# Hybrid backbone layer on one core: the output projection's operand is stored already split in high and low parts

## The chip, the cores and the metric

The kernel runs on one core of one Trainium2 chip. The metric is the device time of one execution in microseconds. TensorE does the matrix products, VectorE (DVE in the rows) and ScalarE (ACT) the elementwise work, GpSimd (POOL) some elementwise work and some DMA issues, SyncE (SP) nearly all DMA issues. Both weights and activations lie in DRAM as float32.

## The reference, cut to what matters

One layer over 1024 latent tokens and 256 context tokens of width 1024. Of the first of its two sub-layers, the change touches the end:

```python
lru_l, lru_c = rglru_mixer(...)                       # (1, 1024, 1024)
ssd_l, ssd_c = ssd_mixer(...)                         # ends in rms_norm(y * silu(z), norm_g)
x = x + g1 * (jnp.concatenate([lru_l, ssd_l], axis=-1) @ lp['w_out'])   # w_out: (2048, 1024)
```

Before that, one input projection feeds both mixers: an LRU (a convolution, gates, and a linear recurrence in both directions, times a GeLU gate) and an SSD (a chunked state-space scan in both directions). After it comes a gated feed-forward part with a convolution of width 3, and a final norm. All of it is computed in float32.

## The kernel before, in words

A float32 product is made of three products of a faster format, `float32r`: an operand is split into a high part (a ScalarE copy into `float32r`, line 144) and a low part (VectorE's difference of the operand and the high part, line 145), and high x high, high x low and low x high are added in PSUM. The helper is `split`. Whoever reads an operand for products therefore pays a ScalarE and a VectorE pass over it.

The work runs in stages, on a TensorE that has something to do in most of them. The times are those of the profiled execution.

- **LRU stage** (to about 490 us): 8 steps `i`, each 128 channels over all tokens. Products with `w_in` give the mixer's input and its gate; convolution (`conv4`), split into `xh` and `xl`, products for the gates (line 432), scans; then line 458 multiplies by the GeLU gate `gg`, and line 460 stores `gg` (128 channels x 1024 tokens) into the DRAM tile `mixd`, ordered by chunks of 128 tokens. Between the steps VectorE reduces adaLN weights (`ada_col`, line 180), each 512 KB, through the ring `wraw` of three buffers that also serves the weights.
- **SSD preparation** (490 to about 742 us): the remaining columns of `w_in`, convolution, decays.
- **SSD stage** (about 742 to 941 us): for two groups of heads and 8 chunks each, states, scores and outputs (`diag`, `chunk_out`, `fwd`), which VectorE chains together. It ends each chunk by storing the gated output into the DRAM tile `gd` (line 778). As filler, `out_lru` runs beside it: the LRU half of the output projection, one column half `h` (512 columns) after the other.
- **SSD projection**: `out_half(1, 0, ...)` (about 941 to 985 us) and `out_half(1, 1, ...)` (about 985 to 1046 us), the SSD half of the output projection for the first and second 512 columns. The second also normalises the new stream (`post`) and prepares the operands `b11`, `t1`, ... of the feed-forward part.
- **Feed-forward part** (from about 1074 us) with two large products made by a Strassen-like scheme.

`out_half(half, h, src, nxt, order)` is what the change rewrites. It makes 8 weight blocks (`out_prep`: a load of 256 KB through the ring, a scaling on VectorE in lines 671 or 673, a split into `oh` and `ol`, nine buffers each, at a high priority). Then it goes over 8 chunks of 128 tokens, the first two as a pair. For each chunk it loads 512 KB of `mixd` or `gd` (through the ring; the first pair of the SSD half through the two `x1` buffers, line 685), and for each half `kq` of it (four blocks of 128) splits 128x512 into `mh` and `ml` and makes 12 products (lines 709 to 711). `mh` and `ml` have four buffers each in the LRU half, in a pool of the SSD stage, and two each in the SSD half. As each column half goes over all chunks, each mixer output is loaded twice and split twice: 2 x 2 x 8 x 2 = 64 splits of 128x512.

The framework that builds the program orders the instructions of each engine by priority in a model of its own; so work of one stage appears beside that of another. Each engine, and each DMA queue, then runs its list in order: an instruction or DMA issue that waits holds what stands behind it. A buffer is reused when the last reader of its former content is done.

The trace prints tiles without their numbers: `x<-gd` is the load of an `x1` buffer, `h<-h,h` one of `post`.

Of the kernel before, what the change touches and what calls it, by code (L numbers as in the profile page):

```python
# [7 lines left out]
FT = mybir.dt.float32  # L8
FR = mybir.dt.float32r
# [6 lines left out]
P = 128  # L16
D = 1024
KD = 8
T = 1024
NCL = 8  # L20
# [30 lines left out]
def backbone_kernel(ctx: ExitStack, tc: tile.TileContext, x, ctxt, vec, rows, ada, ada_t, w_in, w_dt,  # L51
                    gw, w_out, w_up, w_down, out, dbg=None):
    nc = tc.nc
# [6 lines left out]
    ring = ctx.enter_context(tc.tile_pool(name="ring", bufs=2))  # L60
    dram = ctx.enter_context(tc.tile_pool(name="dram", bufs=1, space=DRAM))

    mixd = dram.tile([NCL, P, KD, P], FT, name="mixd")
    gd = dram.tile([NCL, P, KD, P], FT, name="gd")
    zd = dram.tile([NCL, P, D], FT, name="zd")
    xd = dram.tile([NCH, P, D], FT, name="xd")
# [26 lines left out]
    for nm, op in (("gt", OP.is_lt), ("lt", OP.is_gt), ("le", OP.is_ge), ("ge", OP.is_le)):  # L93
        m = m2[:, 0 if nm == "le" else 1, :] if nm in ("le", "ge") else const.tile([P, P], FR, name="m_" + nm)
# [38 lines left out]
    def load_w(src, n=1024):  # L133
        raw = ring.tile([P, 1024], FT, name="wraw", bufs=3)[:, :n]
        nc.sync.dma_start(raw, src)
        return raw
# [3 lines left out]
    def split(hi, lo, src, eng_hi=None):  # L140
        if eng_hi is V:
            V.tensor_copy(hi, src)
        else:
            A.activation(hi, src, AF.Copy)  # L144
        V.tensor_tensor(lo, src, hi.bitcast(FT), op=OP.subtract)  # L145
# [223 lines left out]
    with tc.tile_pool(name="la", bufs=1, reuse_waits="tile") as la, \  # L369
# [21 lines left out]
        for i in range(KD):  # L391
# [46 lines left out]
            for d in range(2):  # L438
# [18 lines left out]
            V.tensor_tensor(hs[0], hs[0], hs[1], op=OP.add)  # L457
            V.tensor_tensor(gg.rearrange("p (c r) -> p c r", r=GR), gg.rearrange("p (c r) -> p c r", r=GR),
                            hs[0].rearrange("p (r c) -> p c r", c=GW), op=OP.mult)
            nc.sync.dma_start(mixd[:, :, i, :].rearrange("c p t -> p c t"), gg.rearrange("p (c t) -> p c t", t=P))  # L460

            ada_cols(i, 2, 5)

# [214 lines left out]
    mpool = [None]  # L678

    def out_half(half, h, src, nxt, order=tuple(range(NCL))):  # L680

        m0 = []
        for c in order[:2] if half else ():
            m0.append(ow.tile([P, D], FT, name="x1", bufs=2))
            nc.sync.dma_start(m0[-1], src[c].rearrange("p a b -> p (a b)"))
        for k in range(len(wts), KD):
            out_prep(half, h, k)
        mine = wts[:]
        wts.clear()
        for cs in [order[0:2]] + [(c,) for c in order[2:]]:  # L690
            mr = m0 or [load_w(src[c].rearrange("p a b -> p (a b)")) for c in cs]
            m0 = []
            po = [fpa.tile([P, 512], FT, name="pa" if c % 2 else "pb", bufs=2) if half
                  else ops.tile([P, 512], FT, name="pf", bufs=2) for c in cs]
            for kq in range(2):
                hl = []
                qs = slice(kq * 512, (kq + 1) * 512)
                for c, m in zip(cs, mr):
                    mp, nb = (ow, 2) if half else (mpool[0], 4)
                    mh = mp.tile([P, 512], FR, name="mh", bufs=nb)  # L700
                    ml = mp.tile([P, 512], FR, name="ml", bufs=nb)
                    split(mh, ml, m[:, qs])
                    hl.append((mh, ml))
                for j in range(4):
                    k = kq * 4 + j
                    oh, ol = mine[k]
                    for (mh, ml), p_ in zip(hl, po):
                        a, b = mh[:, j * P:(j + 1) * P], ml[:, j * P:(j + 1) * P]
                        PE.matmul(p_, a, oh, start=k == 0, stop=False)
                        PE.matmul(p_, a, ol, start=False, stop=False)  # L710
                        PE.matmul(p_, b, oh, start=False, stop=k == KD - 1)
            if nxt and cs[0] == order[-1]:
                out_prep(nxt[0], nxt[1], 0)
            for c, p_ in zip(cs, po):
                yield c, p_
# [555 lines left out]
```

## Time and profile before

| what | value |
|---|---|
| median of 3 runs | 1775.61 us (1767.23 to 1783.1) |
| the profiled execution | 1780.98 us |
| its span | 1779.2 us |
| TensorE products busy | 1624.8 us (91%) |
| VectorE busy | 1418.1 us (80%) |
| ScalarE busy | 931.2 us (52%) |
| GpSimd busy | 445.8 us (25%) |
| moved by DMA | 238.78 MB, mean 134 GB/s |

Busy shares are averages over stages with different limits, so a stage has to be looked at by itself. Matrix products are pipelined: a TensorE that is busy all the time may still issue them at different rates, and its idle time is what the other engines cost it. The idle time of any other engine costs nothing by itself. The granted clock of TensorE is a share of 2.4 GHz.

### The profile page before, as it was taken

How to read it: one execution, taken by the hardware profiler on the slowest of the kernel's cores; microseconds unless marked ns; L12 is line 12 of the kernel's file. 1: busy time of each engine (PE TensorE's matmuls, PEld its weight loads, DVE VectorE, ACT ScalarE, POOL GpSimd, SP SyncE). 2: the span in 40 equal slices, each digit the busy share in tenths (PEclk: the TensorE clock that was granted, in tenths of full speed). 3: DMA queues.
4: the chain of work that ended last, by engine and by line, in shares of the span. 5: the costliest groups of instructions: out<-in, count | busy, mean ns of one | idle time of the engine just before them, and what ended most of it. 6: DMA issues, size and time to landing. Idle time of an engine off the chain costs nothing.

```text
span 1779.2 us, 21578 instructions
## 1 busy us (share of the span) xinstructions
PE 1624.8 (91%) x7682; PEld 1311.9 (74%) x7682; DVE 1418.1 (80%) x1966; ACT 931.2 (52%) x1408; POOL 445.8 (25%) x335
## 2 busy tenths in 40 slices
PE   2889999999999999699999969899999999999996
PEld 2468787887977677476677757788888888888885
DVE  2777878786566668889895699899999999879787
ACT  3548786867746666422323573343443443445445
POOL 0000000000037767332120035445545444200000
PEclk8999999998999999899899988999999999999998
DMA  6615324241213222476756531222322223594433
GB/s 150 234 50 165 100 84 148 88 138 29 79 65 104 95 101 101 165 246 208 249 174 219 197 129 65 89 101 101 124 101 95 101 101 113 183 366 137 165 101 107
DMA packets 106764, 238.78 MB, mean 134 GB/s; under 512 B 10528, under 2 KB 33184, under 8 KB 106656
## 3 DMA queue, kind: packets, MB, share of 16 engines
q1 hardware_dynamic: 105136, 233.73, 39.7%
q0 software_dynamic: 1520, 3.67, 0.6%
q8 instruction: 60, 0.98, 0.2%
q14 instruction: 48, 0.39, 0.1%
HBM read 176.55 MB, written 60.82 MB: 133 GB/s over the span
## 4 chain that ended last, share of the span: by engine, by line
PE 40%; DVE 7%; DMA 3%; ACT 2%; issue 2%; POOL 0%; SPq 0%; POOLq 0%; DVEq 0%; ACTq 0%
PE pd L848 2%; PE pd L846 2%; PE pd L847 2%; PE pc L848 2%; PE pc L847 2%; PE pc L846 2%; PE pa L846 2%; PE pa L847 2%; PE pa L848 2%; PE pdn L1107 2%; PE pdn L1105 2%; PE pdn L1106 2%; DMA wraw<-in_w_out 2%; PE pb L846 1%; PE pb L847 1%
## 5 line engine op out<-in xcount | busy, mean ns | idle before, releaser
L558 POOL TENSOR_TENSOR rh<-m,dah 128x512 fp32r<-128x512 f32 x64 | 74.3, 1160 | 565.5 <-ACT dah L144 503.8
L159 PE MATMUL pl<-hh,whi 128*128 128x512 f32 x416 | 167.6, 403 | 2.2 <-ACT gg L414 1.9
L161 PE MATMUL pl<-hh,wlo 128*128 128x512 f32 x416 | 165.6, 398 | 0.8 <-DVE wlo L145 0.8
L160 PE MATMUL pl<-hl,whi 128*128 128x512 f32 x416 | 165.0, 397 | 0.0
L1023 DVE SCALAR_TENSOR_TENSOR cen<-u,vt,cen 128x1008 f32<-128x1008 f32 x192 | 155.3, 859 | 11.6 <-ACT cen L1019 11.6
L144 ACT ACTIVATE sh<-wraw 128x512 fp32r<-128x512 f32 x158 | 98.5, 624 | 105.7 <-PE pd L847 52.7
L145 DVE TENSOR_TENSOR sl<-wraw,sh 128x512 fp32r<-128x512 f32 x158 | 132.6, 840 | 0.0
L965 POOL TENSOR_TENSOR ssum<-wraw 128x512 f32<-128x512 f32 x48 | 70.5, 1469 | 169.8 <-DVE sl L145 147.8
L144 ACT ACTIVATE sh<-ssum 128x512 fp32r<-128x512 f32 x96 | 59.8, 627 | 101.3 <-PE pc L847 64.4
L144 ACT ACTIVATE sh<-b 128x512 fp32r<-128x512 f32 x80 | 50.6, 632 | 107.0 <-PE pdn L1106 55.3
L159 PEld LDWEIGHTS pl<-hh,whi 128*128 128x128 f32 x416 | 80.0, 192 | 19.5 <-ACT gg L414 2.1
L161 PEld LDWEIGHTS pl<-hh,wlo 128*128 128x128 f32 x416 | 79.7, 192 | 18.0 <-DVE wlo L145 2.0
L160 PEld LDWEIGHTS pl<-hl,whi 128*128 128x128 f32 x416 | 80.2, 193 | 17.2 <-issue 1.0
L1019 ACT ACTIVATE cen<-u,vt 128x1024 f32<-128x1024 f32 x48 | 59.8, 1245 | 59.7 <-DVE u L1012 32.2
L145 DVE TENSOR_TENSOR sl<-ssum,sh 128x512 fp32r<-128x512 f32 x96 | 81.7, 853 | 3.4 <-ACT sh L144 3.4
L383 PE MATMUL pl<-whi,hh 128*128 128x256 f32 x256 | 73.8, 288 | 8.8 <-DVE xc L356 5.7
L558 POOL TENSOR_TENSOR rh<-m,dal 128x512 fp32r<-128x512 f32 x64 | 77.6, 1212 | 0.0
L145 DVE TENSOR_TENSOR sl<-b,sh 128x512 fp32r<-128x512 f32 x80 | 56.0, 701 | 26.6 <-ACT sh L144 26.5
L384 PE MATMUL pl<-wlo,hh 128*128 128x256 f32 x256 | 73.4, 287 | 1.2 <-DVE wlo L145 1.2
L144 ACT ACTIVATE mh<-wraw 128x512 fp32r<-128x512 f32 x56 | 34.9, 629 | 75.3 <-PE pf L710 45.3
L385 PE MATMUL pl<-whi,hl 128*128 128x256 f32 x256 | 73.1, 285 | 0.0
L180 DVE SCALAR_TENSOR_TENSOR wraw<-wraw,silr 128x1024 f32<-128x1024 f32 x32 | 39.1, 1222 | 38.7 <-DMA wraw<-in_ada_t 38.6
(440 smaller groups left out, 5179.6 us busy)
## 6 DMA issues: line engine op xcount, KB each, us to landing
wraw<-in_w_up SPq DMA_DIRECT2D x48, 512.0 KB
wraw<-actd SPq DMA_DIRECT2D x42, 512.0 KB
wraw<-in_w_in SPq DMA_DIRECT2D x36, 512.0 KB
actd<-cen SPq DMA_DIRECT2D x33, 512.0 KB
wraw<-in_ada_t SPq DMA_DIRECT2D x32, 512.0 KB
b<-in_w_down SPq DMA_DIRECT2D x24, 512.0 KB
xk<-xd SPq DMA_DIRECT2D x38, 256.0 KB
ddd<-wd SPq DMA_DIRECT2D x32, 256.0 KB
```

Of the source, the lines that this page charges most:

```text
L144: A.activation(hi, src, AF.Copy)
L145: V.tensor_tensor(lo, src, hi.bitcast(FT), op=OP.subtract)
L159: PE.matmul(ps, wh[:, k, :], hh[k][:, t0:t0 + n], start=k == 0, stop=False)
L160: PE.matmul(ps, wh[:, k, :], hl[k][:, t0:t0 + n], start=False, stop=False)
L161: PE.matmul(ps, wl[:, k, :], hh[k][:, t0:t0 + n], start=False, stop=k == KD - 1)
L383: PE.matmul(o, hh[k][:, t], wh[:, k % 4, :], start=k == 0, stop=False)
L384: PE.matmul(o, hh[k][:, t], wl[:, k % 4, :], start=False, stop=False)
L558: G.tensor_tensor(rh, m[:, None, :].to_broadcast([P, 4, P]), sv[:, :, None].to_broadcast([P, 4, P]), op=OP.mult)
L846: PE.matmul(ps, a[0][:, ks], b[0][:, k, :], start=k == 0, stop=False)
L847: PE.matmul(ps, a[0][:, ks], b[1][:, k, :], start=False, stop=False)
L848: PE.matmul(ps, a[1][:, ks], b[0][:, k, :], start=False, stop=k == 3)
L1023: V.scalar_tensor_tensor(cen[:, o:o + m], uu[:, i_:i_ + m], w_, cen[:, o:o + m], op0=OP.mult, op1=OP.add)
```

## The change

The DRAM tile `mixd` gets a leading index for the two parts, and a new tile `gsd` of the same kind is made for the SSD outputs.

In the LRU stage, `gg` is split after line 458: the high part goes to a new tile `ghi`, the low part into `gg` itself, and two stores replace one. In the LRU half of `out_half` a chunk's two parts are loaded whole, 128x1024 each, into `mh` and `ml`, with two buffers each (before: four of half the width), with no split.

In the SSD half, the first column half loads and splits as before; each part is then also stored to `gsd` by a DMA that GpSimd issues, four of 256 KB for a chunk. The second column half loads the parts from `gsd`: chunks at even places into the two buffers of `mh` and of `ml`, by four loads of 256 KB; the chunk at place 1 into the two `x1` buffers, and the chunks at places 3, 5 and 7 into two of the ring's three buffers, by two loads of 512 KB. The loads of the first two chunks stand ahead of the weight blocks in the program.

So 64 splits of 128x512 become 16 of that size and 8 of 128x1024.

```diff
--- before.py
+++ after.py
@@ -60,7 +60,8 @@
     ring = ctx.enter_context(tc.tile_pool(name="ring", bufs=2))
     dram = ctx.enter_context(tc.tile_pool(name="dram", bufs=1, space=DRAM))
 
-    mixd = dram.tile([NCL, P, KD, P], FT, name="mixd")
+    mixd = dram.tile([2, NCL, P, KD, P], FT, name="mixd")
+    gsd = dram.tile([2, NCL, P, D], FT, name="gsd")
     gd = dram.tile([NCL, P, KD, P], FT, name="gd")
     zd = dram.tile([NCL, P, D], FT, name="zd")
     xd = dram.tile([NCH, P, D], FT, name="xd")
@@ -457,7 +458,10 @@
             V.tensor_tensor(hs[0], hs[0], hs[1], op=OP.add)
             V.tensor_tensor(gg.rearrange("p (c r) -> p c r", r=GR), gg.rearrange("p (c r) -> p c r", r=GR),
                             hs[0].rearrange("p (r c) -> p c r", c=GW), op=OP.mult)
-            nc.sync.dma_start(mixd[:, :, i, :].rearrange("c p t -> p c t"), gg.rearrange("p (c t) -> p c t", t=P))
+            ghi = lw.tile([P, T], FR, name="ghi")
+            split(ghi, gg.bitcast(FR), gg)
+            for e, t in ((0, ghi.bitcast(FT)), (1, gg)):
+                nc.sync.dma_start(mixd[e, :, :, i, :].rearrange("c p t -> p c t"), t.rearrange("p (c t) -> p c t", t=P))
 
             ada_cols(i, 2, 5)
 
@@ -679,28 +683,64 @@
 
     def out_half(half, h, src, nxt, order=tuple(range(NCL))):
 
+        def halves(n, c):
+
+            if half and not h:
+                raw = m0.pop(0) if m0 else load_w(src[c].rearrange("p a b -> p (a b)"))
+                for kq in range(2):
+                    qs = slice(kq * 512, (kq + 1) * 512)
+                    m = [ow.tile([P, 512], FR, name="m" + e, bufs=2) for e in "hl"]
+                    split(*m, raw[:, qs])
+                    for e in range(2):
+                        nc.gpsimd.dma_start(gsd[e, c][:, qs], m[e].bitcast(FT))
+                    yield m
+                return
+            if half and n % 2 == 0:
+                ms = [[ow.tile([P, 512], FR, name="m" + e, bufs=2) for e in "hl"] for _ in range(2)]
+                for kq, m in enumerate(ms):
+                    for e in range(2):
+                        nc.sync.dma_start(m[e].bitcast(FT), gsd[e, c][:, kq * 512:(kq + 1) * 512])
+                yield from ms
+                return
+            if not half:
+                m = [mpool[0].tile([P, D], FR, name="m" + e, bufs=2) for e in "hl"]
+            elif n == 1:
+                m = [ow.tile([P, D], FT, name="x1", bufs=2).bitcast(FR) for _ in "hl"]
+            else:
+                m = [ring.tile([P, 1024], FT, name="wraw", bufs=3).bitcast(FR) for _ in "hl"]
+            for e in range(2):
+                nc.sync.dma_start(m[e].bitcast(FT), gsd[e, c] if half else
+                                  src[e, c].rearrange("p a b -> p (a b)"))
+            for kq in range(2):
+                yield [t[:, kq * 512:(kq + 1) * 512] for t in m]
+
         m0 = []
-        for c in order[:2] if half else ():
+        for c in order[:2] if half and not h else ():
             m0.append(ow.tile([P, D], FT, name="x1", bufs=2))
             nc.sync.dma_start(m0[-1], src[c].rearrange("p a b -> p (a b)"))
+        its = {}
+
+        def begin(n):
+            its[n] = halves(n, order[n])
+            if h or not half:
+                its[n] = iter([next(its[n]), next(its[n])])
+
+        if half and h:
+            begin(0)
+            begin(1)
         for k in range(len(wts), KD):
             out_prep(half, h, k)
         mine = wts[:]
         wts.clear()
-        for cs in [order[0:2]] + [(c,) for c in order[2:]]:
-            mr = m0 or [load_w(src[c].rearrange("p a b -> p (a b)")) for c in cs]
-            m0 = []
+        for ns in [(0, 1)] + [(n,) for n in range(2, NCL)]:
+            cs = [order[n] for n in ns]
+            for n in ns:
+                if n not in its:
+                    begin(n)
             po = [fpa.tile([P, 512], FT, name="pa" if c % 2 else "pb", bufs=2) if half
                   else ops.tile([P, 512], FT, name="pf", bufs=2) for c in cs]
             for kq in range(2):
-                hl = []
-                qs = slice(kq * 512, (kq + 1) * 512)
-                for c, m in zip(cs, mr):
-                    mp, nb = (ow, 2) if half else (mpool[0], 4)
-                    mh = mp.tile([P, 512], FR, name="mh", bufs=nb)
-                    ml = mp.tile([P, 512], FR, name="ml", bufs=nb)
-                    split(mh, ml, m[:, qs])
-                    hl.append((mh, ml))
+                hl = [next(its[n]) for n in ns]
                 for j in range(4):
                     k = kq * 4 + j
                     oh, ol = mine[k]
```

## Rows read from the trace of the kernel before

**Rows 1.** Windows of five stretches: engines' busy time, instructions, granted clock, DMA.

```profile
core 0: us, PE busy (x) PEld busy (x) DVE busy (x) ACT busy (x) POOL busy (x), PEclk, DMA share, GB/s
150.00:490.00 340.00, 317.31 (x1807) 276.14 (x1806) 257.12 (x245) 254.25 (x262) 0.00 (x0) 0.97 0.32 102
742.00:941.00 199.00, 185.62 (x851) 134.35 (x852) 173.56 (x267) 61.66 (x120) 45.11 (x36) 0.95 0.67 217
941.00:985.00 44.00, 40.75 (x179) 32.75 (x178) 22.59 (x39) 16.43 (x32) 0.00 (x0) 1.00 0.67 225
985.00:1046.00 61.00, 55.72 (x259) 44.59 (x258) 46.07 (x95) 40.69 (x101) 3.27 (x2) 0.97 0.58 199
1046.00:1074.00 28.00, 13.01 (x51) 8.73 (x49) 27.03 (x45) 16.47 (x39) 10.19 (x7) 0.72 0.14 48
```

**Rows 2.** Groups by line, 150 to 490: busy us, mean ns, idle before.

```profile
L180 DVE SCALAR_TENSOR_TENSOR wraw<-wraw,silr 128x1024 f32<-128x1024 f32 x27 | 33.0, 1221 | 32.1 <-DMA wraw<-in_ada_t 32.0
...
L145 DVE TENSOR_TENSOR wlo<-wraw,whi 128x1024 fp32r<-128x1024 f32 x21 | 25.8, 1229 | 10.7 <-ACT whi L144 10.7
...
L144 ACT ACTIVATE whi<-wraw 128x1024 fp32r<-128x1024 f32 x21 | 22.1, 1053 | 21.9 <-PE pl L385 17.2 <-PE pg L160 4.7
```

**Rows 3.** The waits of TensorE, 150 to 490: total us, times, longest.

```profile
PE pg L432 <- ACT xh L144: 10.1, 3, 4.4
```

**Rows 4.** The groups by line, 742 to 941.

```profile
L145 DVE TENSOR_TENSOR ml<-wraw,mh 128x512 fp32r<-128x512 f32 x32 | 26.1, 831 | 5.6 <-ACT mh L144 5.1 <-PE pf L710 0.5
...
L144 ACT ACTIVATE mh<-wraw 128x512 fp32r<-128x512 f32 x32 | 19.8, 627 | 52.8 <-PE pf L710 45.3 <-DMA wraw<-mixd 4.5 <-DMA gd<-gt 3.0
```

**Rows 5.** The waits of TensorE, 742 to 941.

```profile
PE pst L775 <- DVE yy L771: 6.2, 5, 3.0
```

**Rows 6.** The chain of waits, 838 to 852: start, duration, what.

```profile
843.31 4.92 DMA wraw<-in_w_out
...
848.25 1.12 DVE wraw L673
...
849.40 0.63 ACT oh L144
850.03 0.53 ACT mh L144
...
850.60 0.80 PE pf L709
```

**Rows 7.** The chain of waits, 885 to 900.

```profile
889.50 5.43 DMA x<-gd
```

**Rows 8.** The tile actd: issue ns min/median/max, first and last start; landing.

```profile
L1039 POOL DMA_DIRECT2D actd<-cen x1: 746/746/746, 1547.1 to 1547.1; - x1
...
DMA to landing us min/median/max: 3.3/5.8/5.9
```

**Rows 9.** The groups by line of ScalarE, 941 to 985.

```profile
L144 ACT ACTIVATE mh<-wraw 128x512 fp32r<-128x512 f32 x12 | 7.6, 631 | 18.6 <-PE pb L710 12.7 <-ACT tq L837 3.9 <-PE pa L710 2.0
```

**Rows 10.** The DMA issues that GpSimd makes: KB each, median us to landing.

```profile
out<-b POOLq DMA_DIRECT2D x4, 512.0 KB, 7.3
actd<-cen POOLq DMA_DIRECT2D x3, 512.0 KB, 5.8
```

**Rows 11.** The groups by line of VectorE, 1022 to 1046.

```profile
L145 DVE TENSOR_TENSOR ml<-wraw,mh 128x512 fp32r<-128x512 f32 x6 | 4.1, 683 | 0.1
```

**Rows 12.** The waits of TensorE, 941 to 1046.

```profile
PE pb L709 <- ACT mh L144: 2.7, 2, 2.3
PE pb L711 <- DVE ml L145: 2.5, 2, 1.6
PE pa L709 <- ACT mh L144: 1.8, 1, 1.8
PE pa L711 <- DVE ml L145: 1.6, 1, 1.6
```

## The prediction

> **What bounds the kernel now.** I first read where the change acts: the split of mixer outputs runs in four stretches, so I cut the span into them and took each engine's busy time [rows 1]. TensorE is the fullest engine in the first four, but not in the same way. In the LRU stage (150 to 490 us) it is busy 317.31 of 340 us, VectorE 257.12, ScalarE 254.25. In the SSD stage, which carries the LRU half of the output projection as filler (742 to 941), TensorE has 185.62 of 199 us and VectorE 173.56: two engines close to full, with the DMA engines at 0.67. In the first column half of the SSD projection (941 to 985) TensorE has 40.75 of 44 and VectorE only 22.59. In the second (985 to 1046) TensorE has 55.72 of 61, VectorE 46.07. Then, from 1046 to 1074, TensorE falls to 13.01 of 28 and VectorE is at 27.03: it bounds the passage into the feed-forward part. The question for each stretch is therefore not how much work leaves VectorE and ScalarE, but which TensorE idle time that work ends.
>
> The profiled execution took 1780.98 us, 1.8 of it outside the span of 1779.2; the median of the runs is 1775.61. I make the sum as a difference on the profiled execution and put it on the median.
>
> **Part 1: the LRU stage gets the splits.** Each of its 8 steps gains a ScalarE copy and a VectorE subtraction of 128x1024; the same shapes take 1053 and 1229 ns for weights [rows 2]. That is 8.4 us of ScalarE and 9.8 us of VectorE in 340. Two stores replace one, 8 more on SP's queue. The cover is VectorE's idle time before the adaLN reductions, 32.1 us, nearly all waiting for their weights' transfers [rows 2]. Where the cover is gone, the added pair delays the next step's convolution and its split, for which TensorE already waits 10.1 us in 3 waits [rows 3]; then all of it counts, 8 x (1.05 + 1.23) = 18 us. Below, the bound is 0, since the stage only gains work. The scheduler puts the convolution ahead and the gated output's work into gaps, so I take about 0.5 us per step: **+4 us** (0 to +18).
>
> **Part 2: the SSD stage loses 32 splits.** They are 19.8 us of ScalarE and 26.1 us of VectorE [rows 4]. TensorE idles 199 - 185.62 = 13.4 us, so that is the most that can be won. Of its waits, 6.2 us are for VectorE's last product before the transposes [rows 5]; with 26.1 of 173.56 us gone from VectorE I take about half, 3 us. The largest single gap is at the change from the first to the second column half [rows 6]: the last `w_out` block is loaded (4.92 us), scaled, split into `oh`, and only behind that, on ScalarE's queue, stands the mixer split `mh` for which the product at 850.60 waits. Without it the products of the blocks already split need not stand behind the last block. But a new wait takes its place: a chunk's parts now need both of two buffers, which come free when the products of the chunk two places before end, not when a split ends. The parts of the second chunk of the new pair can then be asked for only at about 842, and a 512 KB load took 5.43 us in this stage [rows 7]: they are there at about 847.5, so some 3 us of the 850.60 are won. The same limit costs at the start, where four loads (2.1 MB, 6.5 us at the 324 GB/s worked out below) must follow the end of the work that held the pool's room, some 2 us later than the first product now. I count 16 more loads on SP's in-order queue as covered, because the parts need no split behind their landing; what stands behind a blocked one are the loads of x, z and the decays, for which VectorE waits. Their 8.4 MB bring the stage's 43 MB (217 GB/s x 199 us) to 52 MB, at 217 / 0.67 = 324 GB/s some 160 us of 199: no bound on average. Another 2 us I give to VectorE being less in the way elsewhere. Sum -3 - 3 + 2 - 2 = **-6 us** (-13.4 to +8: the last where both pair loads, 13 us, lie on the path and only 5 us of gains come).
>
> **Part 3: the first half of the SSD projection stores its parts.** Its 16 splits stay. Added are 32 stores of 256 KB, issued by GpSimd, which is idle here [rows 1]. An issue occupies GpSimd 0.75 us [rows 8], 4 per chunk 3.0 us, while a chunk takes TensorE 44 / 8 = 5.5 us [rows 1]: the queue keeps up. What matters is the wait: each buffer of parts (two of each kind) is now free for the next split only once its store has landed, and ScalarE, which waits there, holds behind it the squares for the norm and the weight splits. A buffer's turn is the copy, 0.63 us [rows 9], plus issue to landing. It is free of charge up to 5.5 - 0.63 = 4.9 us, less some 0.2 us of signalling, so 4.7 us. No 256 KB store of GpSimd stands in the trace: those of 512 KB took 3.3 to 5.9 us, and 7.3 for the output [rows 8, 10]. At half the size I take 4 to 5 us, just at the limit, since the DMA share here would go from 0.67 to about 0.9 with 4.2 MB more: **+2 us**. Bounds: 0 if landings stay near 3.3; at 7.3 each of 7 turns costs 7.3 - 4.7 = 2.6 us, +18.
>
> The page "DMA: Bandwidth & Descriptors" of the Trainium skill (Anatomy of one DMA) gives a GpSimd DMA about 2.0 us plus the bytes over 436 GB/s, an estimate of 2.6 us for 256 KB. By that this part would cost 0 and the sum would be 2 us lower; the rows for 512 KB, all longer than its 3.2 us, speak against relying on it.
>
> **Part 4: the second half loads what was stored.** 16 splits go, 10.9 us of VectorE and 10.1 of ScalarE at the row's 0.68 and 0.63 us [rows 9, 11]. TensorE's waits for such splits from 941 to 1046 sum to 8.6 us in four rows [rows 12]; about two thirds lie in this half (61 - 55.72 = 5.3 us idle). Six of the subtractions fall into the last stretch before 1046, 4.1 us [rows 11], where VectorE runs on into the passage and is full there [rows 1], so those shorten the passage too. Given back: 24 loads instead of 8 on SP, 4.2 MB more at a DMA share of 0.58, and the first chunk's parts can only be loaded once the first half's last buffers are free, where both chunks of the pair were loaded ahead before. A load of 5.43 us [rows 7] against weights that are being prepared in the same time costs 1 to 2 us. -3 -3 or -4 +1 or +2: **-5 us** (-10 to +5).
>
> Sum: +4 - 6 + 2 - 5 = -5 us, on the profiled execution 1776, on the median 1771 (-0.3%).
>
> **Rivals.** *VectorE was the real bound.* If the 26.1 us that leave it in the SSD stage end all of TensorE's idle time there (-13.4), the second half and the passage win their full -10, and the LRU stage hides its additions, the sum is -13.4 - 10 + 2 = -21: 1754. For it: VectorE's 173.56 of 199. Against: 13.4 us is all idle time, some of it is start-up. Chance 0.17.
> *The stores land too late* (the other side). At the 5.8 us of the three actd stores, 7 x 1.1 = 8 us, at 7.3 us 18, in place of +2; with the rest as above +1 to +11: 1777 to 1787, decided by whether landings pass 4.7 us. Where part 4's gain does not come either, 1792. Chance 0.14.
> "SBUF — State Buffer" of the Trainium skill (SBUF: two separate sides) has a way to it: VectorE operations in a two-port mode keep GpSimd from writing descriptors. It infers that `tensor_tensor` doesn't, and that is what the splits are; no run here shows a store beside such work.
> *The LRU stage pays in full*: +18 instead of +4, sum +9: 1785. For it: TensorE's waits on that very chain. Chance 0.09.
> *The loads of the SSD stage block SP's queue*: +8 instead of -6, sum +9: 1785. For it: doubled loads and in-order waits. Chance 0.06.
> *Nothing moves*, because the new order on the engines gives back what is won: 1776. Chance 0.04; the forecast keeps 0.50.
>
> **How the numbers follow.** The forecast's own range is 1761 to 1781, some 10 us either way for the four estimates. To hold 8 in 10 the range takes in most of the first rival and of the slower ones: 1752 to 1791. A measurement of this kernel can tell about 1% (17.8 us) from no change. Faster by more than that, under 1758: most of the first rival and a little of the forecast, 0.19. Slower, over 1793: only two of the slower rivals together reach it (1771 + 14 + 14 and up to 1771 + 16 + 14), and a cost that none of them names, 0.11. Within: 0.70.
>
> **What would show it.** Part 1: TensorE's wait for `xh` stays near 10 us. Part 2: the stretch ends some 6 us shorter, the gap before 850.60 is halved, and VectorE falls to about 147 us. Part 3: the stretch stays within 2 us of 44 and landings under 4.7 us; ScalarE waiting for `gsd` stores would show the second rival. Part 4: waits for `mh` and `ml` vanish and the passage starts about 5 us earlier relative to the first half's end. A new wait of TensorE on loads of parts over 5 us anywhere would make the prediction wrong.

## The result and the profile after

The changed kernel takes 1804.25 us (median of 4 runs, 1800.59 to 1806.64) against 1779.03 for the kernel before beside it: the ratio is 1.0147, with a 95% interval of 1.0121 to 1.0174. It is slower by some 26 us, and 1804 lies outside the predicted range of 1752 to 1791. The profiled execution took 1800.59 us (span 1798.8), 19.6 us more than that of before.

Six windows of the changed kernel, cut at events that both kernels have: the end of the first and of the last of VectorE's products with the GeLU gate (the LRU stage), the end of the second copy of `cT` (the end of the SSD preparation), the first product of the SSD projection, the seventh product of its second column half, the last product `pa<-b11h,ol` (from the feed-forward part's first products, which stand behind the second half's last), and the first store of activations. Line numbers after are higher by 1 from line 64 of the kernel before, and by 4 and more from its line 461.

```profile
core 0: us, PE busy (x) PEld busy (x) DVE busy (x) ACT busy (x) POOL busy (x), PEclk, DMA share, GB/s
163.30:484.60 321.30, 298.35 (x1662) 258.99 (x1661) 242.59 (x227) 236.46 (x245) 0.00 (x0) 0.98 0.35 109
484.60:753.00 268.40, 226.57 (x1046) 175.23 (x1045) 185.53 (x235) 158.42 (x282) 160.08 (x138) 0.92 0.28 93
753.00:944.00 191.00, 180.26 (x851) 131.66 (x850) 149.50 (x228) 41.03 (x84) 46.78 (x40) 0.99 0.82 276
944.00:1006.00 62.00, 51.77 (x199) 38.74 (x198) 27.95 (x48) 18.77 (x39) 15.07 (x28) 0.93 0.90 311
1006.00:1067.50 61.50, 56.09 (x254) 45.19 (x253) 34.89 (x78) 32.80 (x87) 3.65 (x3) 0.93 0.72 235
1067.50:1125.20 57.70, 37.25 (x152) 29.33 (x151) 50.51 (x74) 26.04 (x48) 28.14 (x18) 0.79 0.17 57
```

The same cuts of the kernel before lie at 172.9, 488.9, 745.6, 941.3, 992.3, 1050.2 and 1104.6 us of its span:

| stretch | before | after | difference | forecast |
|---|---|---|---|---|
| start to the first gated product | 172.9 | 163.3 | -9.6 | none |
| LRU stage | 316.0 | 321.3 | +5.3 | part 1: +4 |
| SSD preparation | 256.7 | 268.4 | +11.7 | none |
| SSD stage | 195.7 | 191.0 | -4.7 | part 2: -6 |
| first half of the SSD projection | 51.0 | 62.0 | +11.0 | part 3: +2 |
| second half | 57.9 | 61.5 | +3.6 | part 4: -5, |
| passage to the feed-forward part | 54.5 | 57.7 | +3.2 | with the passage |
| rest | 674.6 | 673.6 | -1.0 | none |

The cuts of the SSD projection lie some us behind the true ends of its halves. Cut at the first product of each half and at the end of the second's last, the three stretches take 47.5, 56.4 and 59.5 us before and 59.9, 57.5 and 63.8 after: +12.3, +1.2 and +4.4. So what is lost behind the first half is lost in the passage more than in the second half. The text keeps the cuts of the table.

The first row has no changed work in it; it differs between executions (163.3 to 172.9 us over the profiles of this study). Without it the change costs 29 us: 17 around the LRU stage, 11 in the first half, 7 behind it, less 5 in the SSD stage. Answering to [rows 4], the trace shows 2 splits of 128x512 there instead of 32; to [rows 3], TensorE waits 7.3 us for `xh` instead of 10.1. The gap of [rows 6] is nearly gone: from the last product of the first column half to the first of the second it is 849.9 to 853.2 us (before 836.5 to 850.6).

In the place of [rows 12] stand these waits, 944 to 1006 us and then 1006 to 1067.5 (waiting operation, what it waited for, total, times, longest); the third fence is the group of the tile `gsd`, its issues on GpSimd and SP, who waited for it, and the landings of the stores:

```profile
PE pa L751 <- DVE ml L146: 4.6, 2, 3.1
PE pb L749 <- DMA mh<-gsd: 2.5, 1, 2.5
PE pb L749 <- ACT mh L145: 1.9, 3, 0.9
PE pb L751 <- DVE ml L146: 1.0, 1, 1.0
```

```profile
PE pb L749 <- DVE x L949: 3.0, 1, 3.0
PE pt L899 <- DVE x L955: 1.1, 1, 1.1
PE pa L751 <- DMA wraw<-gsd: 1.0, 1, 1.0
```

```profile
L695 POOL DMA_DIRECT2D gsd<-mh x16: 539/542/786, 925.6 to 996.8; - x16
L695 POOL DMA_DIRECT2D gsd<-ml x16: 539/539/559, 937.7 to 999.0; - x16
...
  ACT mh L145: 17.1, 7
  DVE ml L146: 12.0, 6
...
DMA to landing us min/median/max: 2.4/5.5/8.0
```

ScalarE stood 17.1 us and VectorE 12.0 us behind stores that had not landed, and the products waited for their splits.

### The profile page after: what moved, and what is told of

Same layout as the page of the kernel before. It is cut to its first block, busy times and chain, and to the rows that moved or that the text cites. A ratio compares the mean times of both kernels' runs of the same rounds, so it can differ in the third digit from the quotient of the medians.

```text
span 1798.8 us, 21599 instructions
## 1 busy us (share of the span) xinstructions
PE 1630.0 (91%) x7682; PEld 1316.2 (73%) x7682; DVE 1398.7 (78%) x1926; ACT 906.6 (50%) x1364; POOL 463.0 (26%) x367
## 4 chain that ended last, share of the span: by engine, by line
PE 44%; DVE 7%; DMA 5%; issue 4%; POOL 4%; ACT 2%; SPq 0%; POOLq 0%; DVEq 0%; ACTq 0%
POOL rh L562 3%; DMA wraw<-in_w_out 2%; PE pd L887 2%; PE pd L886 2%; PE pd L888 2%; PE pc L887 2%; PE pc L888 2%; PE pc L886 2%; PE pa L887 2%; PE pa L888 2%; PE pa L886 2%; PE pdn L1145 2%; PE pdn L1147 2%; PE pdn L1146 2%; PE pb L886 1%
## 5 line engine op out<-in xcount | busy, mean ns | idle before, releaser
L1063 DVE SCALAR_TENSOR_TENSOR cen<-u,vt,cen 128x1008 f32<-128x1008 f32 x192 | 151.5, 839 | 10.9 <-ACT cen L1059 10.9
L146 DVE TENSOR_TENSOR wlo<-wraw,whi 128x1024 fp32r<-128x1024 f32 x37 | 50.2, 1360 | 23.5 <-ACT whi L145 23.4
L181 DVE SCALAR_TENSOR_TENSOR wraw<-wraw,silr 128x1024 f32<-128x1024 f32 x32 | 39.1, 1221 | 34.4 <-DMA wraw<-in_ada_t 34.2
```

What stands on the lines that cost most here:

```text
L1063: V.scalar_tensor_tensor(cen[:, o:o + m], uu[:, i_:i_ + m], w_, cen[:, o:o + m], op0=OP.mult, op1=OP.add)
```

## The experiments

In each, a stretch means one of the table. The median of the kernel before, beside the runs, was 1774.43 to 1778.51 us.

### Which half of the change loses

**LRU part alone** (against the changed kernel; the SSD half is that of the kernel before):

```
-            if half and not h:
+            if half:
...
-                    for e in range(2):
-                        nc.gpsimd.dma_start(gsd[e, c][:, qs], m[e].bitcast(FT))
```

**SSD part alone** (the LRU half loads and splits `mixd` as before):

```
-            split(ghi, gg.bitcast(FR), gg)
...
-            if half and not h:
+            if not (half and h):
```

> The LRU part of the change alone: split stores in the LRU stage, loads of parts in the SSD stage; the SSD half of the output projection as in the kernel before. Theory: the change loses at three places, (a) the copy of the last LRU step's high part stands on ScalarE ahead of the evacuation that the dt chain needs, 9 to 17 us, (b) the SSD stage gains 5, (c) the SSD projection and the passage behind it lose 9.5 + 4 + 4 = 17.5. This kernel keeps (a) and (b): 1779 + 9 to 17 - 5 = 1783 to 1791. Rival, the load on the DMA engines as a whole: this kernel adds 12.6 of the 21 MB, so 0.6 of the 25 us, 1794, and it would lose in the SSD stage too. Rival, the LRU part costs nothing and the whole loss is in the SSD projection: 1774.

> The SSD part alone: the first column half stores its parts, the second loads them; LRU stage, its store and the SSD stage as in the kernel before. Theory: (c) alone, 1779 + 17.5 = 1796, with the first half of the SSD projection near 59 us instead of 50, and the passage late. Rival DMA load as a whole: 8.4 of 21 MB, 0.4 of 25 us, 1789. Rival, the whole loss lies here: 1804 or over.

Measured: 1787.51 us, ratio 1.0053 (1.0025 to 1.0081), and 1792.46 us, 1.0102 (1.0075 to 1.0128). Together 1.55%, about the change's 1.47%. By stretch, the LRU part has LRU stage and SSD preparation at 588.2 us (before 572.7), the SSD stage at 191.5 (195.7), and the two halves and the passage within 1 us of before; the SSD part has 571.2, 198.2, then 62.0, 59.1 and 57.4 for the two halves and the passage. The SSD part's total lies halfway between its theory (1796) and the rival of the DMA load (1789), so the stretches decide: both parts lose, each in its own, and the one with fewer bytes loses more. The rivals fall.

### What loses in the LRU part

Until the eighth convolution the LRU part runs level with the SSD part, whose LRU stage is unchanged (it starts at 420.1 and 420.7 us): seven steps' splits cost nothing. All of it is lost in the last step and behind it. My first reading was the place of the last copy on ScalarE:

```
-            split(ghi, gg.bitcast(FR), gg)
+            split(ghi, gg.bitcast(FR), gg, V if i == KD - 1 else None)   # whole change otherwise
```

> The changed kernel with one edit: the high part of the last LRU step (of eight) is copied by VectorE instead of ScalarE. If that copy's place on ScalarE's queue is what holds the evacuation of dt, the wait of TensorE for the conversion of dt (8.8 us) goes, and the time is 1804 - 9 to 17 = 1787 to 1795. If the end of the LRU stage is bound by something else (VectorE's chain of the last step, a transfer), nothing moves, 1804, or it is 1 us slower since VectorE has one more copy.

Measured: 1804.31 us, 1.0156 (1.0133 to 1.0179); TensorE's wait for the conversion of dt (from which the SSD decays are made) stayed at 8.6 us. That theory fell. What differs earlier is ScalarE's list in the last step (start, duration, then as before). The kernel before does the first direction's gate ahead of the last `z` columns (`zs`):

```profile
445.15 1.63 ACT L435 ACTIVATE g_r<-pg,vt 128x512 f32<-128x512 f32 x3
447.54 1.37 ACT L443 ACTIVATE th<-g_r,sp 128x1280 f32<-128x1280 f32 x1 [0.77 <-DVE th L457]
...
460.86 1.02 ACT L388 ACTIVATE zs<-pl 128x1024 f32<-128x1024 f32 x1 [0.52 <-PE pl L385]
```

The changed kernel has the copy `ghi` there and all four gates behind `zs`, so both directions follow one another at the end:

```profile
438.50 1.06 ACT L145 ACTIVATE ghi<-gg 128x1024 fp32r<-128x1024 f32 x1 [5.66 <-DVE gg L459]
...
447.35 1.02 ACT L389 ACTIVATE zs<-pl 128x1024 f32<-128x1024 f32 x1 [0.52 <-PE pl L386]
...
453.56 1.63 ACT L436 ACTIVATE g_r<-pg,vt 128x512 f32<-128x512 f32 x3
```

The framework that orders the work had chosen another order. Two kernels with the LRU part alone bring the old list of ScalarE back, one with all eight copies on VectorE, one with copy and subtraction on GpSimd:

```
-            split(ghi, gg.bitcast(FR), gg)
+            split(ghi, gg.bitcast(FR), gg, V)                  # first kernel
+            nc.gpsimd.tensor_copy(ghi, gg)                     # second kernel
+            nc.gpsimd.tensor_tensor(gg.bitcast(FR), gg, ghi.bitcast(FT), op=OP.subtract)
```

> The LRU part of the change alone, with the high part of all eight steps copied by VectorE instead of ScalarE (the run before with this done for the last step alone changed nothing). In the LRU-only run the eight steps cost nothing, but the last one loses its early gate: ScalarE no longer works on the first direction while the last z columns are made, and the end of the scans is 8 us late, the SSD preparation 15 us. In this kernel the list of ScalarE's instructions up to the end of the LRU stage is that of the kernel before. Theory, the order is the loss: the last gated product comes back to 315 to 317 us behind the first (322 without), what is left is the last step's copy and subtraction ahead of dt on VectorE, 2 to 3 us, less the 4 us that the SSD stage wins: 1772 to 1776. Rival, the added VectorE work is the loss: it has 8 x 0.7 = 5.6 us more of it here, 1788 to 1793. Rival, the doubled stores are the loss: 1787.

> The LRU part alone, with both instructions of the split (copy and subtraction) on GpSimd, which has nothing to do in the LRU stage. ScalarE's and VectorE's lists are as before up to the SSD stage. Theory, order: nothing is left of the LRU stage's loss, and the SSD stage wins its 4: 1770 to 1773, about 0.2% under the kernel before. Rival, the doubled stores and the longer way of gg to DRAM hold the next step's buffers: 1780 or over. Rival, GpSimd's work slows VectorE: the scans and reductions of the LRU stage show longer durations and the first 320 us grow by some us.

Measured: 1782.36 us, 1.0032 (1.0008 to 1.0056), and 1787.81, 1.0068 (1.0048 to 1.0087). With VectorE the LRU stage takes 313.4 us, as the order's theory has it (322.4 with ScalarE's copies), but the total missed its 1772 to 1776: its runs lie between 1769.65 and 1786.95, the profiled one lowest, and the SSD preparation still takes 266.6 us. On GpSimd the stage takes 319.4: the copies slow down where VectorE works (minimum, median, maximum in ns).

```profile
L461 POOL CAST ghi<-gg x8: 1039/1846/3217, 168.7 to 488.2; 128x1024 fp32r<-128x1024 f32 x8
```

VectorE's reductions of line 180 went from 1221 to 1290 ns in that kernel. "SBUF — State Buffer" of the Trainium skill (SBUF: two separate sides) has VectorE and GpSimd share one pair of ports that one of them can hold for a whole instruction; these durations agree, though no run here tells the ports from another cause.

The second loss is a place in memory. The changed kernel's trace shows one instruction of the SSD preparation that waits for the store of `ghi`: its tiles take over the LRU stage's room, so the framework puts the chain of dt (softplus, decays) behind the last split.

```profile
488.83 1.21 ACT L342 ACTIVATE xc<-pl,vt 128x1024 f32<-128x1024 f32 x1 [1.92 <-DMA mixd<-ghi]
```

So the last step's high part was put into `g1row`, a row tile that is written much later (and is now declared ahead of the LRU stage); once with all copies on VectorE, once with them on ScalarE:

```
-            ghi = lw.tile([P, T], FR, name="ghi")
+            ghi = lw.tile([P, T], FR, name="ghi") if i < KD - 1 else g1row.bitcast(FR)
```

> The LRU part alone, high parts copied by VectorE, and the last step's high part in another place: in the row tile g1row, which is written only much later, instead of the LRU stage's pool, whose room the first SSD tiles take over. In the three LRU runs so far the 26 to 28 us around dt were 4 to 6 us longer than before although the scans were on time in one of them; there the transposes for dt and VectorE's addition behind them stand after the last split in every list. Theory, room: xst and xc of the SSD preparation lie where ghi lies, so they wait until its split and its store are done, and the framework puts dt behind them; with ghi elsewhere the stretch from the last gated product to the end of SSD preparation falls from 266 us to 257 to 260 (before: 257), the SSD stage keeps its gain, and the time is 1766 to 1771, under the kernel before. Rival, VectorE's own 1.9 us for the last split delay dt wherever it lies: as the run with VectorE copies, 1776 to 1783.

> As the run before it, but with the high parts on ScalarE as in the change: the room alone is changed. Theory, two separate losses (order of the last step's gates, 7 us, and the room, 5 to 8 us): the scans end at 321 to 323 us behind the first gated product, as in the change, and the stretch behind them is that of the kernel before; 1779 to 1782. If the room is no loss: 1787, as the LRU part alone. If it was all of the loss: 1770.

Measured: 1776.25 us, 0.9988 (0.9971 to 1.0005), and 1786.13, 1.0044 (1.0027 to 1.0061). TensorE's wait for dt's result, one line each of the changed kernel, then ScalarE and `g1row`, VectorE and the old place, VectorE and `g1row`:

```profile
PE pg L514 <- DVE xst L505: 8.8, 1, 8.8
```

```profile
PE pg L513 <- DVE xst L504: 6.3, 1, 6.3
```

```profile
PE pg L513 <- DVE xst L504: 3.2, 1, 3.2
```

```profile
PE pg L513 <- DVE xst L504: 0.5, 1, 0.5
```

Before, it was 0.3. The two causes add: about 2.6 us of the wait for the room, 5.7 for the order. From the first gated product to the first half of the SSD preparation's end (the first copy of `cT`) the four take 460.4 (LRU part alone), 457.3, 452.2 and 450.4 us, before 446.1: order 7 to 8, room 2 to 3, and 4 us that no run here places. The last kernel is level with the kernel before and 1.6% under the changed one (1.0147 / 0.9988); no version here beats the kernel before. In the totals the room shows with VectorE's copies alone (1.0032 to 0.9988); with ScalarE's, 1.0053 and 1.0044 can't be told apart, and there it is shown in the wait and the stretch. Both totals are 4 to 5 us over what I expected: the one on ScalarE has its LRU stage at 321.2 us as expected, but its SSD stage at 196.2, with no gain. VectorE's own 1.9 us are out as the cause of the wait, since they are in both kernels with copies on VectorE.

### What loses in the first half of the SSD projection

The changed kernel with the second half as in the kernel before, but the stores kept:

```
-            if half and not h:
+            if half:
...
-                    for e in range(2):
+                    for e in range(0 if h else 2):
```

> The changed kernel, but the second column half of the SSD projection loads the unsplit chunks and splits them as before; the first half still stores its parts, which nobody reads. If the stores' landings hold the first half's buffers and the loads of parts cost the second half and the passage another 8 us, this one keeps the first half's 59 us and wins the 8: 1796. If the stores are all of the loss in the SSD projection: 1804. If the loads of parts are a gain that is hidden behind the late first half (as predicted, 5 us): 1809.

Measured: 1798.78 us, 1.0126 (1.0095 to 1.0157); the first half takes 59.4 us, second half and passage 57.6 and 54.5, as before. So the stores cost the first half 8 to 11 us, and the loads cost 4 to 7 behind it (116.5 us with the SSD part alone, 119.2 in the changed kernel, against 112.4). This is read from the stretches; the interval of the total overlaps that of the changed kernel (1.0121 to 1.0174).

The kernel before with 32 added stores, from a tile that isn't rewritten, and from the parts but 64 of 512 columns:

```
+                    if half and not h:
+                        for e, t in enumerate((mh, ml)):
+                            nc.gpsimd.dma_start(gsd[e, c][:, qs], g1row[:, qs])          # first
+                            nc.gpsimd.dma_start(gsd[e, c][:, kq * 512:kq * 512 + 64],
+                                                t.bitcast(FT)[:, :64])                   # second
```

> The kernel before with 32 stores added in the first column half of the SSD projection: same size and queue as those of the change, but their source is a tile that isn't rewritten, so no buffer of parts waits for a landing. Nobody reads them. Where the stores with their real source are in, that half took 59.4 us (stores alone) and 62 us, against 51. If the hold of the buffers until the landing is the loss: 51 to 53 us, 1775 to 1777 in all. If the traffic itself is (loads of chunks and weights come later): 59 us, 1783.

> The kernel before with the 32 stores of the change's first half from their real source, but each only 64 of 512 columns (32 KB instead of 256). Nobody reads them. Every buffer waits for its store as in the change. If landings are late because of the bytes on busy DMA engines, they come to 2 to 3 us here and the half takes 51 to 53 us: 1775 to 1777. If a GpSimd store holds its buffer for long whatever its size, or its issue is the cost: 58 us or over, 1782.

Measured: 1786.08 us, 1.0058 (1.0038 to 1.0079), and 1776.89, 1.0015 (1.0001 to 1.0029). The first doesn't tell what it was made for: as its stores depended on nothing late, the framework put them at 569.8 to 621.6 us, into the SSD preparation, where GpSimd makes the operands `rh` that TensorE waits for; that stretch grew to 268.9 us. The second is clear: the same buffers wait for the same number of stores, but the half takes 51.1 us, and only one split (VectorE's, 2.9 us) waited for a store. Its landings:

```profile
DMA to landing us min/median/max: 1.7/3.3/5.6
```

To part the hold from the bytes, the same bytes from the unsplit chunk, and the stores of the change issued by SP:

```
+                            nc.gpsimd.dma_start(gsd[e, c][:, qs], m[:, qs])              # kernel before with this
-                        nc.gpsimd.dma_start(gsd[e, c][:, qs], m[e].bitcast(FT))
+                        nc.sync.dma_start(gsd[e, c][:, qs], m[e].bitcast(FT))            # SSD part alone with this
```

> The kernel before with 32 stores of 256 KB added in the first column half of the SSD projection, as many bytes from the same queue at the same places as in the change, but from the unsplit chunk, so the buffers of parts wait for no landing. Nobody reads them. Theory, the hold is the loss: the half takes 51 to 53 us instead of 62, 1777 to 1780. Rival, the traffic is: 58 to 62 us, 1786 or over.

> The SSD part alone with the stores of parts issued by SP instead of GpSimd. If a GpSimd store is late by itself (landings of 5.2 us in the median), SP's land in 3 to 4 us and the first half takes 52 to 55 us, 1785. If the busy DMA engines make them late, landings stay at 5 us, and the half at 60 to 62; where the stores, each waiting for its split, hold loads of chunks and weights behind them on SP, it is longer still, 1792 to 1800.

Measured: 1796.66 us, 1.0098 (1.0073 to 1.0122), with 61.4 us for the half, and 1804.85, 1.0144 (1.0123 to 1.0164), with 68.3. My theory of the hold of the parts' buffers fell: without it, nearly as much is lost. But this kernel has a hold of its own: a store keeps the unsplit chunk's buffer in the ring until it lands, and SP, whose next load wants that buffer, waited for it in the half:

```profile
SPq L136 <- DMA gsd<-wraw: 4.8, 2, 3.8
```

So the bytes without any buffer held were not run. Five windows of 5 us of the kernel that stores the unsplit chunk, and two lines of VectorE's list in it:

```profile
958.50:963.50 5.00, 4.79 (x21) 3.99 (x22) 1.53 (x4) 1.17 (x3) 2.39 (x6) 1.00 1.03 416
963.50:968.50 5.00, 3.66 (x17) 2.69 (x15) 0.00 (x0) 0.63 (x1) 0.52 (x1) 1.00 1.03 385
968.50:973.50 5.00, 0.00 (x0) 0.00 (x0) 1.17 (x2) 0.33 (x1) 2.13 (x4) 0.70 0.75 296
973.50:978.50 5.00, 4.77 (x14) 3.79 (x15) 1.37 (x3) 1.55 (x4) 0.00 (x0) 0.61 0.83 277
978.50:983.50 5.00, 5.00 (x24) 4.14 (x23) 1.77 (x5) 1.64 (x4) 2.14 (x4) 1.00 0.81 240
```

```profile
972.33 0.75 DVE L838 SCALAR_TENSOR_TENSOR xres<-pb,rs,xres 128x512 f32<-128x512 f32 x1 [9.90 <-DMA xres<-x1pd]
973.00 0.68 DVE L146 TENSOR_TENSOR ml<-wraw,mh 128x512 fp32r<-128x512 f32 x1
```

The DMA engines are full for 10 us (share 1.03, up to 416 GB/s; a transfer counts whole in the window in which it starts, so a share can pass 1). A load of the residual `xres` stood on SP behind a load into the ring; that one was issued at 963.3, as soon as a store issued at 954.6 had landed (963.2). The load of `xres`, issued at 964.2, is there only at 972.3; VectorE waits 9.9 us for it, and the split `ml` stands behind it. TensorE stops, and the granted clock, 1.00 (2.4 GHz) until then, is 0.70 and 0.61 in the next windows, a mean of the two levels 1.2 and 2.4 GHz: 14 products where 24 fit. The changed kernel has the same picture at 959 to 974 us, but there the split waits for its buffer's store:

```profile
959.00:964.00 5.00, 4.98 (x23) 3.77 (x21) 0.77 (x2) 2.56 (x6) 1.61 (x3) 1.00 0.97 291
964.00:969.00 5.00, 1.89 (x5) 1.26 (x6) 1.39 (x2) 0.63 (x1) 1.47 (x3) 0.80 1.01 397
969.00:974.00 5.00, 5.00 (x14) 3.91 (x13) 0.75 (x1) 0.00 (x0) 0.67 (x2) 0.52 0.88 262
```

The cause is the bytes of the stores, on DMA engines that five loads of chunks, two of them for the second half, already fill in the kernel before:

```profile
951.30:956.30 5.00, 4.28 (x19) 3.05 (x17) 1.86 (x3) 2.06 (x5) 0.00 (x0) 1.00 0.99 370
```

With the same holds and an eighth of the bytes nothing is lost. The late transfers reach TensorE through buffers that are held until a landing (the parts' or the ring's) and through loads that come late, with the in-order lists of VectorE and SP behind both; how the loss divides between the two is not shown. SP's issue is no way out. Of its 68.3 us, 59.3 lie ahead of the first product of the second half, as with GpSimd's issue (59.4), so the issuing engine is not the cause; the rest comes behind it, where TensorE waits for parts that are loaded late:

```profile
PE pa L745 <- DMA x<-gsd: 5.6, 1, 5.6
```

### What loses behind it

Two kernels with the SSD part alone, and the second of them with the stores of the unsplit chunk:

```
-                m = [ow.tile([P, D], FT, name="x1", bufs=2).bitcast(FR) for _ in "hl"]
+                m = [ring.tile([P, 1024], FT, name="wraw", bufs=3).bitcast(FR) for _ in "hl"]   # first
-        with tc.high_priority(offset=60):
+        with tc.high_priority(offset=400 if c == 7 else 60):                                    # second, third
-                        nc.gpsimd.dma_start(gsd[e, c][:, qs], m[e].bitcast(FT))
+                        nc.gpsimd.dma_start(gsd[e, c][:, qs], raw[:, qs])                       # third
```

> The SSD part alone (1792 in its run), with the second chunk's parts of the second column half loaded into two buffers of the ring instead of the two x1 buffers. In the change TensorE waits 3.0 us there for the epilogue, whose x1 buffers are held by those parts. Theory: that wait goes, the second half and the passage are 3 to 5 us shorter, 1788. Rival: the ring has one buffer left for the eight weight blocks until the pair's products are done, so the second half begins later: 1795 or over.

> The SSD part alone (1792 in its run), with the normalisation of the last chunk put at a higher priority. In the change VectorE takes 14.4 us from the last chunk's residual sum to its scaled stream, against 4.5 before, because splits of the earlier chunks stand in between. Theory: the order on VectorE is what makes the passage 3 us longer: 54 to 55 us from the last product of the half to the first store of activations instead of 57.4, 1789. Rival: the splits that it is put ahead of are needed by the same products, and TensorE starts no earlier: 1792.

> The SSD part alone with the last chunk's normalisation at the higher priority, and with stores from the unsplit chunk in both places of the tile, so that the second half multiplies other values than the parts. The first half is then as in the run before it (51 to 53 us by the theory of the hold), and the second half and the passage show part 4 alone. As predicted (16 splits gone, 5 us won): second half and passage together 107 us, 1774. If the loads of parts win nothing because TensorE's waits only change their source: 112 us as before, 1779. If they lose by themselves: 115 us or more, 1783.

Measured: 1818.52 us, 1.0222 (1.0196 to 1.0248); 1793.09, 1.0084 (1.0054 to 1.0114); 1797.77, 1.0115 (1.0089 to 1.014). The ring is the rival's case, far beyond its bound: the second half takes 79.0 us, with the weight blocks squeezed through one buffer (TensorE waits 5.6 us for `oh`). The priority does what its theory says in its place: in the changed kernel the last chunk's scaling follows its sum after 14.4 us, here after 5.3,

```profile
1069.21 0.74 DVE L949 SCALAR_TENSOR_TENSOR x<-pa,rs,x 128x512 f32<-128x512 f32 x1
...
1079.11 1.65 DVE L146 TENSOR_TENSOR t2l<-h,t2h 128x512 fp32r<-128x512 f32 x1
1080.91 1.52 DVE L146 TENSOR_TENSOR t4l<-h,t4h 128x512 fp32r<-128x512 f32 x1
...
1083.60 1.72 DVE L955 TENSOR_SCALAR x<-x,r_y 128x1024 f32<-128x1024 f32 x1
```

```profile
1060.07 0.74 DVE L943 SCALAR_TENSOR_TENSOR x<-pa,rs,x 128x512 f32<-128x512 f32 x1
...
1065.35 1.75 DVE L949 TENSOR_SCALAR x<-x,r_y 128x1024 f32<-128x1024 f32 x1
```

and the passage takes 54.6 us instead of 57.4, the second half 57.5 instead of 59.1. The totals' intervals (1.0084 and 1.0102) overlap, so it is shown in the stretch and not in the time. Second half and passage together are then 112.1 us, and 114.1 in the third kernel (the same traffic, but no hold of the parts' buffers), against 112.4 before: even with the order mended the loads of parts win nothing.

## Why the prediction was wrong

**Part 1** was right where it looked. The forecast was half a microsecond per step, and seven steps cost nothing. It failed in the sentence that the scheduler puts the convolution ahead "and the gated output's work into gaps", and in the SSD preparation, which had no term: I took the order of the lists as given and priced the work added to it. The last step lost its early gate (7 to 8 us) and the SSD preparation waited for the last split's room (2 to 3). Of the 17 us, 4 to 6 stay without a cause: with both mended (copies on VectorE), LRU stage and SSD preparation take 578.8 us, before 572.7. Neither was a rival; that the sum, +17, still lies under the upper bound of +18 is luck, since that bound was made of a delay in each of eight steps, and seven had none. The SSD preparation needed a term, since tiles that take over a closed pool's room wait for its last reader (`xc` for the store of `ghi`, 1.9 us).

**Part 2** was right in direction and nearly in size: -4.7 for -6. TensorE's wait of [rows 5] fell from 6.2 to 3.6 us, about the half that was said, and VectorE has 149.5 us where about 147 was said. Other terms were off in opposite directions: the gap of [rows 6] nearly vanished where some 3 us of it were to go, and the first of the filler's products stood 9.2 us behind the start of the stretch instead of 2.3, where 2 us more were said. The stretch also varies by several us with the order: 187.3 to 196.2 over the kernels with the LRU part alone, so the closeness is in part luck.

**Part 3** failed at the choice inside its bounds: landings "4 to 5 us, just at the limit" were 5.5 in the median and 8.0 at most, and the half lost 11 us, inside the 0 to +18. The second rival gave its place and its test (ScalarE waiting for `gsd` stores) rightly. The forecast took landings at the limit, and 20 of the 32 passed it (4.7 us). What both lacked is why: I averaged the DMA share to 0.9, where rows of 5 us reach 1.0. "DMA: Bandwidth & Descriptors" of the Trainium skill (Specifications) gives 435 GB/s as the fabric's ceiling; the 416 GB/s agree that there is little room above. Its formula's 2.6 us, weighed in the prediction, is near the shortest landing, 2.4, and far from the median.

**Part 4** failed in its gain. The waits for splits went, and waits for `x1` (3.0 us) and for loads came (1.0, and 2.5 for the first parts, which the table's first half holds); in the passage, where 4.1 us of subtractions were to be saved, the framework put splits of other chunks ahead of the last chunk's normalisation, for which TensorE waits. Where that is mended, the two stretches are level with before, not 5 us shorter.

The sum of the forecast was -5 us; it came out as +29 without the start of the program: against their terms +13 in part 1, +1 in part 2, +9 in part 3, +12 in part 4, and -1 in the rest. The text said that only two slower rivals together would pass 1793, and gave that 0.11; the late stores were one of them, with the mechanism that it names. The other 17 us have the size of the rival in which the LRU stage pays in full, but not its mechanism, and belong to "a cost that none of them names", which stands in the same 0.11.

## What to carry to other kernels

Where a framework orders the lists, adding instructions reprices the order: compare the lists around the last step of a loop, and what lies in the room that its tiles give up, before trusting that filler covers the work. Take the DMA share in windows of the length of a stage's turn, not as its mean, before adding transfers; what saturates first may hold an engine that only shares its list with the work. An idle time that "goes" is won only if what is late next is named.

## What the runs showed of the hardware

A cast of 128x1024 from float32 to float32r takes 0.69 us on VectorE and 1.06 on ScalarE; on GpSimd 1.04 in the two copies with no VectorE instruction beside them, and 1.81 to 3.22 in the six others. A GpSimd store of 32 KB still took 3.3 us to land in the median, one of 256 KB 5.5 with the DMA share at 0.90. An issue on GpSimd took 0.54 us, where the prediction had 0.75. After the stop of TensorE at 967 to 973 us, in the kernel that stores the unsplit chunk, the granted clock was a mean of 0.61 for 5 us, in which 14 products ran where 24 fit at 2.4 GHz: 10 x 5 / 24 = 2.1 us on top of the stop.
